# Layer 0's feed-forward gate and up products for both halves at once by Strassen's algorithm, the down blocks afterwards, and the recurrence's output transposes one chunk later

## The chip, the cores and the metric

The kernel runs on one core of a Trainium2 chip. A core has a matrix engine (TensorE, PE), two elementwise engines (VectorE, DVE, and ScalarE, ACT), a slower one (GpSimd, POOL), and SyncE (SP), which here only issues transfers (DMA). PE reads operands from on-chip memory (SBUF) and adds its products up in PSUM, which has eight banks of 128 x 512 float32. Each engine works through its own list of instructions in order and waits on semaphores. The metric is device microseconds of one execution; several executions are made and their median is given.

## The reference, cut to what matters

The computation is a two-layer trunk on 1024 positions of width 1024, in float32. Layer 0 mixes with a gated spatial mixer and pooling, layer 1 with a recurrence (RWKV-7); each layer has a SwiGLU feed-forward of hidden width 2816, which is 22 blocks of 128.

```python
def swiglu(hn, w_gate, w_up, w_down):
    return (jax.nn.silu(hn @ w_gate) * (hn @ w_up)) @ w_down

def reference(x, ...):
    h = x
    for layer in range(DEPTH):                                  # DEPTH = 2
        hn = rms_norm(h, mix_norm[layer])
        if layer % 2 == 0:
            h = h + hybrid_ab_mixer(hn, ...)
        else:
            y, v_first = rwkv7_time_mix(hn, ...)
            h = h + y
        h = h + swiglu(rms_norm(h, ffn_norm[layer]), ffn_w_gate[layer], ffn_w_up[layer], ffn_w_down[layer])
    return rms_norm(h, final_norm)

def wkv7_scan(r, w, k, v, a, b):                                # inside rwkv7_time_mix
    def step(state, inp):
        r_t, w_t, k_t, v_t, a_t, b_t = inp
        sa = jnp.einsum('bhvk,bhk->bhv', state, a_t)
        state = (state * w_t[:, :, None, :] + sa[..., None] * b_t[:, :, None, :]
                 + v_t[..., None] * k_t[:, :, None, :])
        return state, jnp.einsum('bhvk,bhk->bhv', state, r_t)
    ...
```

The feed-forward and the projections look at each position alone. The recurrence goes through the positions in order.

## The kernel before

**Precision.** Every dense operand is split into a high and a low part (`split`, line 142: ACT makes the high part, DVE subtracts it from the source and rounds the rest). A product is three matmuls, high·high, high·low and low·high (`mm3`, lines 343 to 346), each 128 x 128 by 128 x 512.

**Halves.** The positions are two halves, A (0) and B (1), of 512 columns. The residual stream `H[h]` lies transposed, as eight tiles of 128 features by 512 positions. The recurrence of layer 1 takes half A first and then half B, in eight chunks of 64 positions each.

**Weights.** `plan` lists all blocks of weights (512 KB each) in the order of use, together with the reloads of activations from DRAM. `take` (line 131) hands the next one out, splits it and loads the two after it, through three raw buffers (`raw`, tag of the pool `wst`) and three pairs of split ones. The loads are issued from ACT's queue, other transfers from SP's.

**Feed-forward.** `ffn` (line 648) goes through groups of two or three hidden blocks: for each block the gate product (24 matmuls), the up product (24), SiLU and multiplication and the split of the hidden block; then the down products of the group (24 matmuls per block), whose sums are added to `H` (`residual`, line 423). So each half of layer 0 loads and splits all gate, up and down weights for itself.

**Stages.** After layer 0's mixer: (1) all 22 blocks of half A's feed-forward, with the norm of half B, which is written to DRAM for later (`n_d`), beside it. (2) The first four blocks of half B's, with the splits and mixes for half A's layer-1 projections beside them (`beside`, line 695; `LOWRANK_AT`, `GATE_AT` and `MIX_AT` say from which step the parts come). (3) The projections of half A (`project`, line 896): gate output, keys, receptances, the inversion of the chunks' small triangular matrices on DVE, then values. (4) Half A's recurrence (`recur`, line 1152) with blocks 4 to 19 of half B's feed-forward interleaved (`drive`, line 732, ratio 3), then blocks 20 and 21 while half A's recurrence output is reloaded. (5) Half B's norm and projections, beside half A's output projection and two blocks of layer 1's feed-forward; half B's recurrence beside more of that; the rest.

**The recurrence.** Each chunk is a `burst` (line 1277) of small matmuls, all recorded at line 1176 and kept in their order on PE by `ordered` (line 1172), with ACT and DVE copies between them; within a burst the next chunk's gram products, transposes and small solves are made too. After every second chunk `post` (line 1336) normalises the output of the pair (`bn_stats` on DVE, a power on POOL, 16 ACT instructions, multiplication and addition on DVE and POOL), turns it on PE (line 1384), gates it on DVE (line 1390) and stores it (`y_d`, line 1394).

**Order.** The program is traced in the order of the code; a planner then puts every engine's instructions in order by a priority (the place in the program, 450 places earlier for the interleaved side work), by what is ready in its own model of time, and by what room in the pools is free. A tile's room is taken again when its last reader is done, by later pools too.

## Time and profile before

| | |
|---|---|
| median of 3 runs | 2477.68 us (2475.45 to 2480.0) |
| profiled execution, its own time | 2477.63 us |
| its span, first to last instruction | 2475.9 us |
| PE, DVE, ACT, POOL busy | 97%, 56%, 37%, 10% |
| mean granted clock of TensorE | 0.989 |
| moved by DMA | 310.69 MB, mean 125 GB/s |

The time is a little longer than the span, since it holds what lies around the first and the last instruction. Busy time is the union of an engine's instructions; the duration of one matmul is longer than the distance between two, since they overlap, so for dense work the count in a stretch of time says more than the duration. "Idle before, releaser" in a group says what the engine last waited for. The granted clock is 1.00 at full speed; the profile shows it at half speed for a few microseconds after some gaps in PE's work.

### The profile page before, as it was taken

How to read it: one execution, taken by the hardware profiler on the slowest of the kernel's cores; microseconds unless marked ns; L12 is line 12 of the kernel's file. 1: busy time of each engine (PE TensorE's matmuls, PEld its weight loads, DVE VectorE, ACT ScalarE, POOL GpSimd, SP SyncE). 2: the span in 40 equal slices, each digit the busy share in tenths (PEclk: the TensorE clock that was granted, in tenths of full speed). 3: DMA queues.
4: the chain of work that ended last, by engine and by line, in shares of the span. 5: the costliest groups of instructions: out<-in, count | busy, mean ns of one | idle time of the engine just before them, and what ended most of it. 6: DMA issues, size and time to landing. Idle time of an engine off the chain costs nothing.

```text
span 2475.9 us, 37980 instructions
## 1 busy us (share of the span) xinstructions
PE 2406.4 (97%) x15735; PEld 1977.5 (80%) x15735; DVE 1382.7 (56%) x2126; ACT 912.1 (37%) x1369; POOL 244.6 (10%) x262
## 2 busy tenths in 40 slices
PE   8999999999999998999999999989999999999998
PEld 7888888888878787888878777778878778888887
DVE  6445634444875874655548847856555446444443
ACT  6233422222664432432325754433232324322223
POOL 0200000000014400211000133201111000000001
PEclk9999999999999999999999999999999999999999
DMA  5123433323355577542434465695444322433231
GB/s 179 49 60 89 150 102 102 119 86 94 109 176 139 140 208 202 156 127 70 135 112 143 153 168 134 191 234 140 119 128 128 111 85 75 147 102 118 87 98 56
DMA packets 436396, 310.69 MB, mean 125 GB/s; under 512 B 93376, under 2 KB 395584, under 8 KB 435456
## 3 DMA queue, kind: packets, MB, share of 16 engines
q10 hardware_dynamic: 297280, 210.53, 28.6%
q1 hardware_dynamic: 138944, 97.75, 13.8%
q8 instruction: 123, 2.02, 0.3%
q14 instruction: 49, 0.40, 0.1%
HBM read 254.68 MB, written 53.54 MB: 124 GB/s over the span
## 4 chain that ended last, share of the span: by engine, by line
PE 82%; DMA 6%; DVE 5%; ACT 2%; issue 2%; POOL 2%; SPq 0%; ACTq 0%; POOLq 0%; DVEq 0%
PE mm L344 22%; PE mm L345 22%; PE mm L346 22%; PE sm L1176 5%; DMA raw<-y_d 1%; DVE wlo L144 1%; PE yp L1176 1%; DMA raw<-in_ffn_w_down_dram 1%; DMA lnw<-in_rwkv_ln_w_dram 1%; ACT whi L143 1%; PE aux L1097 1%; PE mm L511 1%; PE mm L512 1%; PE mm L513 1%; PE aux L1098 1%
## 5 line engine op out<-in xcount | busy, mean ns | idle before, releaser
L345 PE MATMUL mm<-alo,whi 128*128 128x512 f32 x1952 | 766.7, 393 | 0.9 <-issue 0.8
L346 PE MATMUL mm<-ahi,wlo 128*128 128x512 f32 x1952 | 765.4, 392 | 1.7 <-DVE wlo L144 1.7
L344 PE MATMUL mm<-ahi,whi 128*128 128x512 f32 x1952 | 765.8, 393 | 0.8 <-ACT whi L143 0.8
L143 ACT ACTIVATE whi<-raw 128x1024 fp32r<-128x1024 f32 x288 | 304.6, 1059 | 744.7 <-PE mm L345 605.3
L144 DVE TENSOR_TENSOR wlo<-raw,whi 128x1024 fp32r<-128x1024 f32 x288 | 359.1, 1248 | 289.5 <-ACT whi L143 270.1
L346 PEld LDWEIGHTS mm<-ahi,wlo 128*128 128x128 f32 x1952 | 367.7, 188 | 82.5 <-issue 3.5
L345 PEld LDWEIGHTS mm<-alo,whi 128*128 128x128 f32 x1952 | 367.7, 188 | 79.9 <-issue 2.9
L344 PEld LDWEIGHTS mm<-ahi,whi 128*128 128x128 f32 x1952 | 367.7, 188 | 79.0 <-issue 2.1
L344 PE MATMUL mm<-hidhi,wdhi 128*128 128x512 f32 x624 | 240.5, 395 | 8.1 <-DVE h L424 3.8
L345 PE MATMUL mm<-hidlo,wdhi 128*128 128x512 f32 x624 | 245.0, 393 | 0.4 <-DVE hidlo L674 0.4
L346 PE MATMUL mm<-hidhi,wdlo 128*128 128x512 f32 x624 | 244.9, 392 | 0.0
L424 DVE TENSOR_TENSOR h<-h,mm 128x512 f32<-128x512 f32 x192 | 129.3, 686 | 149.7 <-PE mm L346 148.5
L143 ACT ACTIVATE wdhi<-raw 128x1024 fp32r<-128x1024 f32 x82 | 86.4, 1057 | 249.7 <-DMA raw<-in_ffn_w_down_dram 164.4
L144 DVE TENSOR_TENSOR wdlo<-raw,wdhi 128x1024 fp32r<-128x1024 f32 x82 | 100.2, 1223 | 112.1 <-ACT wdhi L143 112.0
L670 DVE TENSOR_TENSOR sg<-sg,mm 128x512 f32<-128x512 f32 x88 | 60.3, 686 | 157.1 <-PE mm L346 155.3
L344 PEld LDWEIGHTS mm<-hidhi,wdhi 128*128 128x128 f32 x624 | 117.5, 189 | 36.8 <-DVE h L424 6.4
L345 PEld LDWEIGHTS mm<-hidlo,wdhi 128*128 128x128 f32 x624 | 117.8, 189 | 25.7 <-DVE hidlo L674 1.3
L346 PEld LDWEIGHTS mm<-hidhi,wdlo 128*128 128x128 f32 x624 | 117.8, 189 | 24.9
L424 DVE TENSOR_TENSOR hA<-hA,mm 128x512 f32<-128x512 f32 x72 | 48.8, 686 | 77.2 <-PE mm L346 77.0
L349 POOL TENSOR_TENSOR nrs<-nrs,small 128x4 f32<-128x4 f32 x8 | 10.0, 1244 | 667.2 <-DVE nrs L371 667.2
L674 DVE TENSOR_TENSOR hidlo<-sg,hidhi 128x512 fp32r<-128x512 f32 x88 | 65.7, 748 | 10.0 <-ACT hidhi L673 10.0
L344 PE MATMUL mm<-xhi,whi 128*128 128x512 f32 (+1 forms) x160 | 65.3, 408 | 0.0
(299 smaller groups left out, 2886.3 us busy)
## 6 DMA issues: line engine op xcount, KB each, us to landing
raw<-in_ffn_w_gate_dram ACTq DMA_DIRECT2D x88, 512.0 KB
...
```

Source lines behind the costliest of these rows:

```text
L143: act.activation(hi, src, AF.Copy)
L144: (eng or dve).tensor_tensor(out=lo, in0=src, in1=hi.bitcast(F32), op=ALU.subtract)
L344: pe.matmul(o, whi, xhi, start=first, stop=False)
L345: pe.matmul(o, whi, xlo, start=False, stop=False)
L346: pe.matmul(o, wlo, xhi, start=False, stop=last)
L424: dve.tensor_tensor(out=H[h][:, m, :], in0=H[h][:, m, :], in1=o, op=ALU.add)
L511: pe.matmul(ops[j], xhi[:, k, sl], whi[:, kk], start=(k == 0), stop=False)
L512: pe.matmul(ops[j], xhi[:, k, sl], wlo[:, kk], start=False, stop=False)
L513: pe.matmul(ops[j], xlo[:, k, sl], whi[:, kk], start=False, stop=(k == KT - 1))
L670: dve.tensor_tensor(out=s, in0=s, in1=o, op=ALU.mult)
L674: dve.tensor_tensor(out=lo, in0=s, in1=hi.bitcast(F32), op=ALU.subtract)
L1176: i = f(*args, **kw)
```

## The change

The gate and up products of layer 0 for both halves are taken as one product of 2 x 2 blocks and computed by Strassen's algorithm in Winograd's form, with seven block products in place of eight. Rows of the blocks are the two hidden blocks 2i and 2i+1 of a pair, columns the two halves, and the inner dimension is cut into k-tiles 0 to 3 and 4 to 7. With A the weights and B the normed activations:

S1 = A21+A22, S2 = S1-A11, S3 = A11-A21, S4 = A12-S2; T1 = B12-B11, T2 = B22-T1, T3 = B22-B12, T4 = B21-T2. The products A11·B11 (kept as P1), A12·B21, S2·T2, S1·T1, S3·T3, A22·T4 and S4·B22 are added up partly in PSUM, partly on DVE, to the four results.

- **First part** (`first_steps`): for the pairs 0 to 5 the products P1 and A12·B21 need half A only. They run while DVE makes the T's of `combine`; P1 is stored to DRAM (`p1_d`). Their hidden blocks are finished and stored.
- **Main part** (`full_steps`): all 11 pairs, in the order 6, 0, 7, 1, ... The weights are loaded once for both halves (those of pairs 0 to 5 a second time, half of them), summed and split on DVE and ACT (`weights`, in place in the raw buffers). Pairs 0 to 5 start from the stored P1 and need five products, the others seven. The last two products of a matrix come after the first one or two of the next. PSUM is one pool of eight banks.
- All hidden blocks go to DRAM (`hid_d`), high and low parts; the residual streams too (`hm_d`), since their room is used for the T's.
- **Down blocks** (`down_steps`): 22 for half A in groups of three; for half B four groups of three beside the projections' preparation, then groups of two: two beside half A's recurrence at ratio 28 and three after it, with the reload of its output between them. Hidden blocks come back from DRAM, `H` too.
- The norms of layer 0's feed-forward take running sums of squares as the residuals are made; half B's normed activations aren't stored and reloaded any more.
- **Recurrence**, both halves: `post` first copies the pair's output from PSUM to SBUF on ACT and normalises it there; the transposes, gating and store are put off to the next chunk's burst (`turned`).

```diff
-LOWRANK_AT, GATE_AT, MIX_AT = (5, 8), (7, 8), 2
+LOWRANK_AT, GATE_AT, MIX_AT = (2, 8), (3, 8), (1, 2)
...
-BESIDE = (4, 2)
+BESIDE = 2
+PAIRS = 11
+FIRST = (0, 1, 2, 3, 4, 5)
+PORDER = (6, 0, 7, 1, 8, 2, 9, 3, 10, 4, 5)
...
+        if key[0] in makes:
+            ready[i] = makes[key[0]](i)
+            return
         raw = raws[i]
-        hi, lo = (dest or whl)()
+        to = (dest or whl)()
+        if to is None:
+            return
+        hi, lo = to
...
+    D0A = [list(range(f, min(f + 3, 22))) for f in range(0, 22, 3)]
+    D0B = [[f, f + 1, f + 2] for f in range(0, 12, 3)], [[12, 13], [14, 15]], [[16, 17], [18, 19], [20, 21]]
+    hm_d = [dram.tile([P, KT, HT], F32, name=f"hm_d{h}") for h in range(2)]
+    hid_d = [dram.tile([P, 22, 2, HT], F32, name=f"hid_d{h}") for h in range(2)]
+    p1_d = dram.tile([P, 2 * PAIRS, HT], F32, name="p1_d")
...
+    for i, n in mats(FIRST):
+        push(("first", i, n), push_pair(0, i, n, 0))
+    for i, n in mats(PORDER):
+        for j in range(2):
+            push((f"full{j}", i, n), push_pair(0, i, n, j))
...
+    push_beside(0, [lambda g=g: push_d(0, 1, [g]) for g in D0B[0]])
+    push_proj(0)
+    push_d(0, 1, D0B[1])
+    pieces = push_act(("y", 0), y_d[0])
+    for g in D0B[2]:
+        push_d(0, 1, [g])
+        list(zip(range(2), pieces))
+    list(pieces)
...
+    FULL = {"mm": ("mm", 8)}
...
+    def quarter(o, w, x, start):
+        wh, wl = v3(w[0]), v3(w[1])
+        for k in range(4):
+            st = start and k == 0
+            pe.matmul(o, wh[:, k, :], x[0][:, k, :], start=st, stop=False, skip_group_check=True)
+            pe.matmul(o, wh[:, k, :], x[1][:, k, :], start=False, stop=False, skip_group_check=True)
+            pe.matmul(o, wl[:, k, :], x[0][:, k, :], start=False, stop=k == 3, skip_group_check=True)
...
+    def first_steps(blocks, hn, fp):
...
+        for i, n in blocks:
+            w = take(("first", i, n))
+            o = mmt()
+            quarter(o, parts_of(w, LO), b11, True)
+            t = fp.tile([P, HT], F32, tag="t1", bufs=2, name="p1")
+            act.activation(t, o, AF.Copy)
+            sp.dma_start(p1_d[:, 2 * i + n, :], t)
+            yield 0.5
+            if prev:
+                second(*prev.pop())
+                yield 0.5
+            prev.append((i, n, w, o))
+        second(*prev.pop())
+        yield 0.5
...
+    def full_steps(blocks, kept, x, fp, wp):
...
+        def weights(i):
+            (a11, a12), (a21, a22) = ((raws[j][:, LO], raws[j][:, HI]) for j in (i - 1, i))
+            s3 = wp.tile([P, HT], F32, tag="s3", bufs=1, name="s3")
+            dve.tensor_tensor(out=s3, in0=a11, in1=a21, op=sub)
+            s1, s2, s4 = a21, a11, a12
+            dve.tensor_tensor(out=s1, in0=a21, in1=a22, op=ALU.add)
+            dve.tensor_tensor(out=s2, in0=s1, in1=a11, op=sub)
+            b = whl()
+            split(s2, *parts_of(b, HI))
+            split(s1, *parts_of(b, LO))
+            d = [wp.tile([P, HT], F32R, tag=t, bufs=1, name=t) for t in ("s3hi", "s3lo")]
+            split(s3, *d)
+            dve.tensor_tensor(out=s4, in0=a12, in1=s2, op=sub)
+            c = [wp.tile([P, D], F32R, tag=t, bufs=2, name=t) for t in ("chi", "clo")]
+            split(a22, *parts_of(c, LO))
+            split(s4, *parts_of(c, HI))
+            return b, c, d
...
+        for i, n in blocks:
+            k = i in kept
+            a = mmt()
+            w = take(("full0", i, n))
+            if not k:
+                quarter(a, parts_of(w, LO), x["b11"], True)
+                t1 = tile_("t1")
+                act.activation(t1, a, AF.Copy)
+                yield 0.5
+                o = mmt()
+                quarter(o, parts_of(w, HI), x["b21"], True)
+                dve.tensor_tensor(out=t1, in0=t1, in1=o, op=ALU.add)
+                finish(i, n, 0, t1)
+                yield 0.5
+            b, c, d = take(("full1", i, n))
+            quarter(a, parts_of(b, HI), x["t2"], k)
+            yield 0.5
+            if prev:
+                prev[0]()
+                yield 0.5
+            if k:
+                t1 = tile_("t1")
+                sp.dma_start(t1, p1_d[:, 2 * i + n, :])
+            def now(t, k=k, a=a, t1=t1):
+                if k:
+                    dve.tensor_tensor(out=t, in0=t1, in1=a, op=ALU.add)
+                else:
+                    act.activation(t, a, AF.Copy)
+            u2, u3 = tile_("t2"), tile_("t3")
+            now(u2)
+            o = mmt()
+            quarter(o, parts_of(b, LO), x["t1"], True)
+            yield 0.5
+            if prev:
+                prev[1]()
+                yield 0.5
+            quarter(a, d, x["t3"], False)
+            now(u3)
+            dve.tensor_tensor(out=u3, in0=u3, in1=o, op=ALU.add)
+            finish(i, n, 3, u3)
+            yield 0.5
+            def last(i=i, n=n, k=k, a=a, t1=t1, c=c, now=now):
+                quarter(a, parts_of(c, LO), x["t4"], False)
+                if k:
+                    now(t1)
+                    finish(i, n, 2, t1)
+                else:
+                    finish(i, n, 2, tile_("t4"), a)
+            def last2(i=i, n=n, o=o, u2=u2, c=c):
+                quarter(o, parts_of(c, HI), x["b22"], False)
+                dve.tensor_tensor(out=u2, in0=u2, in1=o, op=ALU.add)
+                finish(i, n, 1, u2)
+            prev = last, last2
+        for go in prev:
+            go()
+            yield 0.5
+    def down_steps(l, h, groups, fp, nw, nh, after=None, between=iter(())):
+        dests["d0"] = lambda: (fp.tile([P, D], F32R, tag="wdhi", bufs=nw, name="wdhi"),
+                               fp.tile([P, D], F32R, tag="wdlo", bufs=nw, name="wdlo"))
+        def load(g):
+            res = {}
+            for f in g:
+                res[f] = fp.tile([P, 2, HT], F32R, tag="hd", bufs=nh, name="hd")
+                sp.dma_start(res[f].bitcast(F32), hid_d[h][:, f])
+            return res
+        nxt = load(groups[0])
+        for gi, g in enumerate(groups):
+            wd, hid = {}, nxt
+            for f in g:
+                if f == groups[-1][-1]:
+                    split_at(pos[0])
+                    dests["d0"] = None
+                wd[f] = take(("d", l, h, f))
+            if gi + 1 < len(groups) and nh >= len(g) + len(groups[gi + 1]):
+                nxt = load(groups[gi + 1])
+            for m in range(KT):
+                o = mmt()
+                ms = slice(m * P, (m + 1) * P)
+                for i, f in enumerate(g):
+                    mm3(o, wd[f][0][:, ms], wd[f][1][:, ms], hid[f][:, 0, :], hid[f][:, 1, :], i == 0, i == len(g) - 1)
+                residual(m, h, o)
+                if after is not None and gi == len(groups) - 1:
+                    after(m)
+                yield len(g) / 8
+            if gi + 1 < len(groups) and nh < len(g) + len(groups[gi + 1]):
+                nxt = load(groups[gi + 1])
+            for _ in range(2):
+                next(between, None)
...
+                if turned:
+                    turned.pop()()
...
-            yp = ypair[0]
+            ysb = wt("ysb", 1, [P, 2, 8, 64])
+            for r in range(2):
+                act.activation(ysb[:, r], ypair[0][:, r], AF.Copy)
...
+            def turn_out():
+                for q in range(2):
...
+                sp.dma_start(y_d[h][:, :, jj * P : (jj + 1) * P], gch)
+            turned.append(turn_out)
...
+        turned.pop()()
+        yield 1.0
...
+    drive(first_steps(mats(FIRST), hnA, f), combine(norm_bcast(acc[0])), 1.6)
+    for e in (rp_es, hb_es, ps_es):
+        e.close()
+    ps_es = open_psum("psf0", FULL)
+    wp, wp_es = open_pool(name="wp", bufs=1, side="left")
+    exhaust(full_steps(mats(PORDER), FIRST, x, f, wp))
+    for e in (wp_es, f_es, xt_es, actp_es, ps_es):
+        e.close()
...
+    for h, pl in ((0, ha_pool), (1, hb_pool)):
+        H[h] = pl.tile([P, KT, HT], F32, tag="h", name="h")
+        sp.dma_start(H[h], hm_d[h])
+    f, f_es = open_pool(name="ffn0d", bufs=1, side="right")
+    acc, add = running_sums(0)
...
-    drive(ffn(0, 0, hnA, f), early_work())
+    drive(down_steps(0, 0, D0A, f, 6, 6, add), wa1())
...
-    beside(0, ffn(0, 1, hnB, f, G0B[0], nd=2, after=spill_b), weights_of(G0B[0]), parts)
+    beside(0, down_steps(0, 1, D0B[0], f, 4, 3, spill_b), [len(g) for g in D0B[0]], parts)
...
-    drive(ffn(0, 1, nxt["hn"], f, G0B[1]), with_reload(hb_pool, 1, h_d[1, 0], recur(0, wp)), RATIO)
+    H[1] = hb_pool.tile([P, KT, HT], F32, tag="h", name="h")
+    for k in range(0, KT, 2):
+        sp.dma_start(H[1][:, k : k + 2, :], h_d[1, 0][:, k : k + 2, :])
+    drive(down_steps(0, 1, D0B[1], f, 3, 4), recur(0, wp), 28.0)
...
-    drive(ffn(0, 1, nxt["hn"], f, G0B[2], after=spill_h, between=take_act(("y", 0))))
+    drive(down_steps(0, 1, D0B[2], f, 3, 4, spill_h, take_act(("y", 0))))
```

## The prediction, made before the change was run

> **What bounds the kernel now.** I read the page first (engine shares, chain of waits), then busy time by stretches of time, then the groups of instructions, then the timeline around the first half's recurrence.

> ```profile
> span 2475.9 us, 37980 instructions
> PE 2406.4 (97%) x15735; PEld 1977.5 (80%) x15735; DVE 1382.7 (56%) x2126; ACT 912.1 (37%) x1369; POOL 244.6 (10%) x262
> PE 82%; DMA 6%; DVE 5%; ACT 2%; issue 2%; POOL 2%; SPq 0%; ACTq 0%; POOLq 0%; DVEq 0%
> ```

> TensorE (PE) is busy 97% of the span, and 82% of the chain that ends last is PE work. So whatever takes matmuls away is worth their time, and whatever uncovers a wait costs its length. What one matmul is worth is not its duration: matmuls overlap.

> ```profile
> L345 PE MATMUL mm<-alo,whi 128*128 128x512 f32 x1952 | 766.7, 393 | 0.9 <-issue 0.8
> 350.00:600.00 250.00, 250.00 (x1104) 207.02 (x1103) 105.20 (x123) 61.31 (x74) 0.00 (x0) 1.00 0.31 95
> ```

> The columns of a stretch are PE, weight load, DVE, ACT and POOL busy time with instruction counts, granted clock, DMA share, GB/s. One matmul lasts 393 ns, but 1104 of them go through 250 us of pure feed-forward work: 0.2264 us each. DVE is at 42% there and ACT at 25%, so this stage has room beside PE. The profiled execution took 2477.63 us, the span plus 1.7; the median of the runs is 2477.68, so the sum below is made from 2477.6.

> **What the change removes.** Layer 0's gate and up products are 22 hidden blocks x 2 matrices x 2 halves x 8 k-tiles x 3 passes (hi·hi, hi·lo, lo·hi) = 2112 matmuls. After it there are 11 pairs x 2 matrices x 7 products x 4 k-tiles x 3 passes = 1848. The down blocks keep 1056. That is 264 x 0.2264 = **-59.8 us**. Bounds: none of the seven products can be skipped, and each is the same 128x512 form, so the count is exact; only its exposure is open.

> **What it adds on DVE and ACT**, beside PE:

> ```profile
> L144 DVE TENSOR_TENSOR wlo<-raw,whi 128x1024 fp32r<-128x1024 f32 x288 | 359.1, 1248 | 289.5 <-ACT whi L143 270.1 <-PE mm L346 6.1 <-PE mm L344 5.0
> L358 DVE TENSOR_TENSOR nacc<-nacc,nsq 128x512 f32<-128x512 f32 x35 | 24.1, 687 | 0.8
> L424 DVE TENSOR_TENSOR h<-h,mm 128x512 f32<-128x512 f32 x192 | 129.3, 686 | 149.7 <-PE mm L346 148.5
> L674 DVE TENSOR_TENSOR hidlo<-sg,hidhi 128x512 fp32r<-128x512 f32 x88 | 65.7, 748 | 10.0 <-ACT hidhi L673 10.0
> 660.00:710.00 50.00, 50.00 (x221) 40.61 (x220) 46.47 (x67) 38.01 (x57) 2.55 (x4) 1.00 0.37 113
> ```

> While the first six pairs run their two products of half A (288 matmuls, 65 us of PE), DVE makes the five activation sums: per k-tile 13 operations of about 0.69, so 52 x 0.69 = 36 us, plus 12 weight splits x 1.25 = 15, plus 6 hidden blocks x 1.43 = 9: 60 us under 65.
> In the main part a matrix of a kept pair has 60 matmuls, 13.6 us. DVE does 4 weight sums (L358's 0.69) and 5 half splits (0.69), 6.2 us, and on the results 5 additions (L424's 0.686) and on average 1.5 x (0.69+0.75), 5.6 us: 11.8, or 87%. A matrix of the other pairs has 84 matmuls, 19.0 us, and 12.5 us of DVE. The last row is a stage of the kernel before in which DVE was busy 93% and PE never idle, so I take **0**, and PE's own work is the cover. The other end: the weights of a matrix need both raw blocks, there are three raw buffers, and the second load waits until the sums of the matrix before are done in place.

> ```profile
> 1172.56 0.35 ACTq L113 DMA_DIRECT2D raw<-in_ffn_w_down_dram  x1
> 1176.15 1.06 ACT L143 ACTIVATE wdhi<-raw 128x1024 fp32r<-128x1024 f32 x1 [2.78 <-DMA raw<-in_ffn_w_down_dram]
> ```

> A load is there 3.6 us after its issue. If DVE did all 11.8 us before it, the cycle would be 15.4 against 13.6, 1.8 x 12 kept matrices = 22 us. Bounds 0 to 22.

> **Hidden blocks by way of DRAM.** 44 stores and 44 loads of 0.52 MB go onto SP's queue; half of the down weights' traffic is doubled. A down group of three is 72 matmuls, 16.3 us, and wants 3.1 MB, 193 GB/s.

> ```profile
> 940.00:950.00 10.00, 6.25 (x54) 4.92 (x54) 2.82 (x5) 2.60 (x3) 0.00 (x0) 0.98 1.14 299
> 720.00:730.00 10.00, 8.37 (x24) 6.26 (x25) 1.23 (x1) 4.74 (x8) 0.00 (x0) 0.66 0.83 248
> ```

> 299 GB/s were moved in one stretch, so steady state fits. The starts do not all fit. At the start of half A's down blocks the residuals H come back from DRAM (2 x 2.1 MB) into the room of the activation tiles, which the last product still reads; the hidden blocks' tiles lie where t4 is read one product (12 matmuls, 2.7 us) earlier. Low end 2 us (hidden blocks issued first, one weight split of 1.06 + 1.25 left). High end 21 us (both H first: 5.8 MB at 299 GB/s, then the split). Nearer the low end, since what is free first can be issued first on SP: **+5**. The residual of the first tile waits for H, and PE has five PSUM tiles, 45 matmuls or 10 us, before that reaches it.
> At half B's first stage there are three hidden-block buffers for groups of three, so the next group's loads start when the group before has been read: 3.6 us for the first and 1.7 for each of two more, 7 us, once; the two later boundaries have the low-rank and gate products (48 matmuls, 10.9 us each) over them. Bounds 0 (low-rank pulled forward) to 2.3 + 2 x 7 = 16. I take **+7**.

> **The clock.** After the idle before 720 us the granted clock was 0.66, and 24 matmuls took 8.37 us in place of 5.4: 2.9 us more. Two new gaps of over 4 us in dense work: **+6**, bounds 0 to 4 gaps, 12.
> [...]

> **The recurrence of half A loses its cover.** This is the largest cost. Before, 16 hidden blocks of half B's feed-forward (1152 matmuls) run beside it, and 2 more after it. Now four down blocks (96 matmuls, 21.7 us) are interleaved at a ratio of 28, and six (144 matmuls, 32.6 us) come after it in program order.

> ```profile
> 900.00:1300.00 400.00, 387.68 (x3946) 320.69 (x3945) 220.47 (x395) 128.21 (x213) 38.24 (x32) 0.99 0.48 137
> 900.00:1200.00 300.00, 89.87 (x2654) 80.74 (x2654) 0.99 0.53 148
> 905.54 0.39 PE L1099 MATMUL mm<-whi,xlo 128*128 128x512 f32 x1
> 960.35 0.24 PE L1176 MATMUL sm<-XT,w 32*32 32x32 f32 x2
> 978.46 0.69 PE L1176 MATMUL sm<-XT,w 32*32 32x32 f32 x32
> 989.75 0.69 PE L1176 MATMUL sm<-XT,gt 32*32 32x32 f32 x32
> 1155.45 1.15 PE L1176 MATMUL yp<-uv,gt 128*64 128x64 f32 x31
> 1162.02 2.91 POOL L349 TENSOR_TENSOR var<-var,small 128x16 f32<-128x16 f32 x1 [38.81 <-DVE var L1362]
> 1165.24 4.83 ACT L1370 ACTIVATE ysb<-yp,mean,var 128x64 f32<-128x64 f32 x16 [15.51 <-DVE mean L1364]
> 1177.44 0.93 PE L1176 MATMUL sm<-ident,ysb 128*128 128x128 f32 x7
> 1181.17 0.53 SPq L1394 DMA_DIRECT2D y_d<-gch  x1
> ```

> The second row counts the recurrence's own instructions (line 1176) alone: 90 us. With 54 us of down blocks the new region holds 144 us of PE work. Its chain of latency: from the last value product (905.5) to the first burst (960.4) 55 us, of which two splits of reloaded activations leave, 52; eight bursts of 12.0 (978.46 to 990.44), 96; from the last product (1156.6) to the issue of the last y (1181.7) 25, less 3.6 for which the transposes stood behind dense matmuls, 21.5; then y's landing, reload and split, 3.6 + 2.3 + about 2: 29 in all. Each earlier pair's normalisation is a 4.83 us block on ACT in front of the next burst's copies; three of them, half hidden: 7. Sum 184, idle 184 - 144 = 40. The region before idled 400 - 387.7 = 12, so **+26 to 28; I take +26**.
> That the output transposes come a chunk later is what keeps the POOL power, the ACT block and the additions (1162.0 to 1173.7) out of the ordered PE chain; without it each pair would add some 12 us. Behind each later transpose nothing waits but the store of y.
> Low end 0: the planner hides as much as before. High end: all four normalisations exposed (+12), and groups 18 to 21, whose weights follow y's pieces in the list of loads, run only after y is there (96 matmuls, +22): 60.
> In the second half's recurrence, which keeps its cover, the later transposes can only free PE from waits, and the norm of half B isn't written out and reloaded any more: **-1**, bounds -5 to +2.

> Sum: -59.8 + 0 + 5 + 7 + 6 + 26 - 1 = -16.8: **2461 us**.

> **Rivals.**
> (1) *All covered.* The list of dense work is filled in wherever PE waits, as in the bursts shown, the region idles 12 us as before, no gap reaches the clock. For it: 97% busy in all stages of before. Against: 144 us of work cannot fill 184. -59.8 + 2 + 2.3 = 2422 us.
> (2) *Slower: the recurrence bare.* Place: from half B's last value product to its first output product. Price 60 in place of 26, the other terms as they are: -59.8 + 60 + 17 = +17, 2495 us. It decides from 43 us in this region. For it: the order of weights and y in one ring of three buffers; the first burst waited for a DMA share above 1.0. Against: PE's order already mixes single matmuls of several stages.
> (3) *Strassen's own feeding binds.* DVE and the raw ring in the kept pairs: +22, 2483 us, about the time of before or a little over. For it: 87% of DVE and a chain of split, sum, split. Against: the stage at 93%.
> That the change does not do what it says is no rival: the matmul count follows from the code.

> **From cases to numbers.** A measurement of this kernel tells about 0.2% (5 us) from no change. Forecast 0.48, its own range 2445 to 2475; (1) 0.18; (2) 0.20; (3) 0.14. Faster: 0.48 x 0.97 + 0.18 + a seventh of (3) = 0.67. Same: nearly half of (3) and the edges of the others, 0.09. Slower: 0.24. The range goes from (1) to (2), 2422 to 2495.

> **What would show it.** PE instructions of the dense kind fall by 264 and the matmul rate in the new stage stays 4.4 per us: the first step right. DVE near 85% with PE never idle in kept pairs: no cost there; PE waiting for DVE weight halves: rival (3). A PE gap before half A's first down product, waiting for H or the hidden blocks, and one between half B's first and second group. From the last value product to the first output product some 185 us with about 40 idle; 155 with 12 is rival (1), 215 or more rival (2). Wrong altogether if the gap is elsewhere, for instance at the value projection or in half B's recurrence, whose instructions hardly change.

## The result, and the profile after

The changed kernel takes 2533.1 us (median of 4 runs, 2527.9 to 2539.0), the kernel before on the same chip 2478.4 (2475.5 to 2480.0): a ratio of 1.0224, 95% interval 1.0203 to 1.0246. It is 55 us slower; 17 us faster was forecast. The profiled execution took 2539.0 us, a span of 2537.3 plus 1.7, against 2477.6 before: 61.4 us more, and it is this difference that the rows below account for.

The page of the changed kernel: the span, and the engines' busy time.

```profile
span 2537.3 us, 38209 instructions
PE 2369.7 (93%) x15471; PEld 1948.5 (77%) x15471; DVE 1493.2 (59%) x2380; ACT 953.1 (38%) x1479; POOL 237.3 (9%) x262
```

There are 264 matmuls fewer, as counted. But busy time fell by 36.7 us where 264 x 0.2264 = 59.8 are gone, so the matmuls that are left take 23.1 us longer; and idle time grew from 69.5 to 167.6 us, by 98.1. -59.8 + 23.1 + 98.1 = +61.4. Two questions follow: where the idle time stands, and why matmuls take longer.

Busy time by stages of the kernel before (columns as in the prediction: PE, weight load, DVE, ACT, POOL, granted clock, DMA share, GB/s): up to half A's gate and up; half A's feed-forward; from half A's norm to its last value product; its recurrence with what runs beside it, up to the first output product; the rest.

```profile
0.00:262.90 262.90, 254.13 (x1144) 207.95 (x1145) 136.76 (x199) 108.50 (x169) 22.11 (x49) 0.99 0.30 94
262.90:628.00 365.10, 365.10 (x1614) 302.04 (x1614) 166.72 (x200) 103.01 (x128) 5.44 (x5) 1.00 0.36 112
628.00:905.90 277.90, 267.00 (x1511) 217.67 (x1510) 209.89 (x336) 147.31 (x216) 61.95 (x63) 0.98 0.53 147
905.90:1307.90 402.00, 389.68 (x3954) 322.13 (x3953) 221.96 (x394) 130.20 (x218) 38.24 (x32) 0.99 0.49 140
1307.90:2475.90 1168.00, 1130.44 (x7519) 927.74 (x7517) 647.40 (x998) 423.07 (x640) 116.82 (x113) 0.99 0.43 126
```

The changed kernel: up to gate and up; the seven products; the gap behind them; half A's down blocks; the hand-over to half B's; half B's blocks beside half A's gates and projections; the recurrence's region; the rest.

```profile
0.00:258.70 258.70, 248.57 (x1126) 203.04 (x1127) 134.22 (x196) 106.89 (x168) 21.08 (x48) 0.99 0.34 110
258.70:685.50 426.80, 422.94 (x1859) 346.98 (x1857) 292.83 (x450) 172.35 (x281) 1.12 (x2) 1.00 0.42 134
685.50:703.30 17.80, 0.21 (x1) 0.24 (x2) 5.43 (x6) 3.58 (x4) 0.00 (x0) 0.63 0.97 369
703.30:825.20 121.90, 121.61 (x528) 100.14 (x528) 64.29 (x83) 22.02 (x23) 5.03 (x4) 0.98 0.55 192
825.20:868.00 42.80, 23.12 (x83) 17.71 (x84) 36.31 (x54) 22.76 (x33) 1.59 (x2) 0.76 0.46 169
868.00:1129.80 261.80, 255.01 (x1464) 208.75 (x1463) 185.22 (x304) 123.28 (x179) 57.75 (x61) 0.99 0.55 158
1129.80:1362.50 232.70, 161.96 (x2898) 137.38 (x2898) 131.43 (x292) 70.27 (x143) 34.28 (x32) 0.84 0.54 163
1362.50:2537.30 1174.80, 1136.23 (x7518) 934.23 (x7516) 643.49 (x1000) 432.00 (x650) 116.48 (x113) 0.98 0.43 126
```

Length minus PE's busy time is the idle time of a stage:

| place | idle before | idle after | difference |
|---|---|---|---|
| up to gate and up | 8.8 | 10.1 | +1.3 |
| the seven products (before: half A's feed-forward) | 0.0 | 3.9 | +3.9 |
| gap before half A's down blocks | none | 17.6 | +17.6 |
| half A's down blocks | none | 0.3 | +0.3 |
| half A's norm, gates, projections; in the changed kernel from the hand-over on | 10.9 | 19.7 + 6.8 | +15.6 |
| half A's recurrence, up to its first output product | 12.3 | 70.7 | +58.4 |
| the rest | 37.6 | 38.6 | +1.0 |

**The seven products** cost next to nothing beside their matmuls: 1859 in 422.9 us are 0.2275 each. Of the 3.9 us of idle time, 3.0 are six waits for the split of S3 on ACT.

**The gap before the down blocks**, first on the queue of SP, then on PE:

```profile
685.09 0.32 SPq L1815 DMA_DIRECT2D h<-hm_d  x1
685.50 0.38 SPq L728 DMA_DIRECT2D hid_d<-hid  x1
685.97 0.38 SPq L1815 DMA_DIRECT2D h<-hm_d  x1
688.24 0.32 SPq L728 DMA_DIRECT2D hid_d<-hid  x1
688.61 7.31 SPq L876 DMA_DIRECT2D hd<-hid_d  x6
```

```profile
703.09 0.76 PE L384 MATMUL mm<-hd,wdhi 128*128 128x512 f32 x1 [17.81 <-DMA hd<-hid_d]
```

Both residuals (`h`, 4.2 MB) are issued ahead of the last hidden block's store and of all hidden blocks' loads (`hd`).

**The hand-over** is what the prediction did not have at all. The kernel before went from half A's feed-forward into half B's, whose activations lay in SBUF. Now the next dense work is half B's down blocks, and they stand behind half A's norm. The waits of PE, 822 to 870 us (total, times, longest):

```profile
PE mm L384 <- ACT ahi L155: 9.3, 1, 9.3
PE aux L419 <- DVE nacc L411: 5.4, 1, 5.4
PE mm L384 <- DMA hd<-hid_d: 3.2, 1, 3.2
PE aux L432 <- DVE ndg L428: 2.1, 1, 2.1
```

In order of time they are the sums of squares (5.4), the norm's spread over the partitions (2.1), the start of half B's first down blocks (9.3) and their second group of hidden blocks (3.2). The 9.3 us are put down to a split of the normalised half A (`ahi`), but the first hidden block ended them. SyncE (SP) waited until DVE had normalised half A (`hn`) before it issued that load:

```profile
SPq L876 <- DVE hn L1057: 8.9, 1, 8.9
```

```profile
841.83 1.27 SPq L876 DMA_DIRECT2D hd<-hid_d  x3
```

The load's last part landed at 845.48 by the semaphore's record in the trace, and PE began at 845.62; the first weight's split was done at 843.1.

**The recurrence's region**: PE's waits from 1129 to 1363 us, and its two largest gaps in the tail, behind the last product of the recurrence (1302.4):

```profile
PE sm L1435 <- DMA bk<-bk_d: 14.0, 1, 14.0
PE mm L384 <- ACT wdhi L155: 12.8, 1, 12.8
PE sm L1433 <- DVE ysb L1638: 11.5, 1, 11.5
PE mm L384 <- DVE h L478: 10.6, 3, 6.3
```

```profile
1313.92 0.44 PE L1433 MATMUL sm<-ident,ysb 128*128 128x128 f32 x1 [11.53 <-DVE ysb L1638]
1332.28 0.79 PE L384 MATMUL mm<-hd,wdhi 128*128 128x512 f32 x1 [12.82 <-ACT wdhi L155]
```

The region takes 232.7 us, against the 184 that the prediction had for its chain and 215 for its worst rival. Behind the last product PE waits for the normalisation, then for down weights that were loaded behind pieces of y, and the last four blocks' 96 matmuls run only then.

**The clock.** Stretches of 3.41 us around the end of the recurrence; behind POOL's count stands the granted clock:

```profile
1294.43:1297.85 3.42, 2.58 (x50) 2.39 (x48) 0.69 (x1) 0.31 (x1) 0.13 (x1) 0.50 0.36 102
1297.85:1301.26 3.41, 3.41 (x70) 3.29 (x68) 0.69 (x1) 0.59 (x1) 0.00 (x0) 0.54 0.31 94
1301.26:1304.67 3.41, 1.13 (x40) 0.99 (x35) 2.84 (x14) 1.09 (x2) 0.00 (x0) 0.96 0.03 7
1304.67:1308.09 3.42, 0.00 (x0) 0.00 (x0) 1.50 (x12) 0.00 (x0) 1.74 (x1) 0.50 0.00 0
...
1331.98:1335.39 3.41, 3.11 (x8) 2.49 (x9) 1.23 (x1) 1.26 (x2) 0.00 (x0) 0.54 0.78 273
1335.39:1338.81 3.42, 2.62 (x12) 1.80 (x10) 2.33 (x2) 1.10 (x2) 0.00 (x0) 1.00 0.76 249
```

Behind a stretch with 1.13 us of PE work the clock is half here (1304.67), and it is full again behind stretches with 3.41 and 3.11 us of work at the slow clock (1301.26, 1335.39); behind one with 2.58 us it stays half (1297.85). The first down products after the tail (1332 to 1335) go at half speed, eight in 3.1 us. In sum the trace has the clock at half for 57 us before and 173 us after, and PE is busy in 46 us of the one and 98 of the other. At half clock one dense matmul follows another after 0.426 us (846.61 to 850.02, eight of them) in place of 0.226, so the 52 us more of slow work hold about 25 us of loss. That is an estimate, but it has the size of the 23 us.

### The profile page after: what moved, and what is told of

It is laid out like the page before. It is cut to its first block, busy times and chain, and to the rows that moved or that the text cites. A ratio compares the mean times of both kernels' runs of the same rounds, so it can differ in the third digit from the quotient of the medians.

```text
span 2537.3 us, 38209 instructions
## 1 busy us (share of the span) xinstructions
PE 2369.7 (93%) x15471; PEld 1948.5 (77%) x15471; DVE 1493.2 (59%) x2380; ACT 953.1 (38%) x1479; POOL 237.3 (9%) x262
## 5 line engine op out<-in xcount | busy, mean ns | idle before, releaser
L384 PE MATMUL mm<-ahi,whi 128*128 128x512 f32 x1248 | 489.1, 393 | 1.8 <-DVE h L478 1.0
L386 PE MATMUL mm<-ahi,wlo 128*128 128x512 f32 x1248 | 489.1, 392 | 1.4 <-DVE wlo L156 1.4
L385 PE MATMUL mm<-alo,whi 128*128 128x512 f32 x1248 | 490.2, 393 | 0.1
L155 ACT ACTIVATE whi<-raw 128x1024 fp32r<-128x1024 f32 (+1 forms) x262 | 256.7, 984 | 556.8 <-PE mm L385 404.2
L156 DVE TENSOR_TENSOR wlo<-raw,whi 128x1024 fp32r<-128x1024 f32 (+1 forms) x262 | 298.7, 1143 | 185.4 <-ACT whi L155 159.2
L384 PEld LDWEIGHTS mm<-ahi,whi 128*128 128x128 f32 x1248 | 234.6, 188 | 52.6 <-issue 1.8
L386 PEld LDWEIGHTS mm<-ahi,wlo 128*128 128x128 f32 x1248 | 234.7, 188 | 52.3 <-DVE wlo L156 2.2
L385 PEld LDWEIGHTS mm<-alo,whi 128*128 128x128 f32 x1248 | 234.7, 188 | 51.4 <-issue 1.9
L384 PE MATMUL mm<-hd,wdhi 128*128 128x512 f32 x352 | 144.4, 411 | 58.1 <-DMA hd<-hid_d 25.5
L385 PE MATMUL mm<-hd,wdhi 128*128 128x512 f32 x352 | 143.0, 406 | 0.0
L386 PE MATMUL mm<-hd,wdlo 128*128 128x512 f32 x352 | 138.0, 398 | 0.0
L715 PE MATMUL mm<-ahi,whi 128*128 128x512 f32 x264 | 103.4, 392 | 0.7 <-ACT p L750 0.7
L716 PE MATMUL mm<-alo,whi 128*128 128x512 f32 x264 | 102.7, 389 | 0.0
L717 PE MATMUL mm<-ahi,wlo 128*128 128x512 f32 x264 | 101.8, 389 | 0.0
```

Of the source, the lines that this page charges most:

```text
L155: act.activation(hi, src, AF.Copy)
L156: (eng or dve).tensor_tensor(out=lo, in0=src, in1=hi.bitcast(F32), op=ALU.subtract)
L384: pe.matmul(o, whi, xhi, start=first, stop=False)
L385: pe.matmul(o, whi, xlo, start=False, stop=False)
L386: pe.matmul(o, wlo, xhi, start=False, stop=last)
L715: pe.matmul(o, wh[:, k, :], x[0][:, k, :], start=st, stop=False, skip_group_check=True)
```

## The experiments

All are variants of the changed kernel (2533.1 us) unless said; ratios are against the kernel before, with 95% intervals. From one kernel to the next line numbers move by a few.

### The gap before the down blocks

`hid_first` moves the text: the hidden blocks' loads, then half A's residuals in four pieces; half B's later.

```
-        sp.dma_start(H[h], hm_d[h])
...
+    pre = load_hid(0, D0A[0], f, 6)
...
+    for k in range(0, KT, 2):
+        sp.dma_start(H[0][:, k : k + 2, :], hm_d[0][:, k : k + 2, :])
...
     def wa1():
         yield 8.0
+        sp.dma_start(H[1], hm_d[1])
```

> Against the changed kernel (2533). Where half A's down blocks start, the hidden blocks of the first group are loaded ahead of the residuals, half A's residuals follow in four pieces, and half B's are loaded later beside the down blocks. Theory A (both residuals first on the queue set the 17.8 us gap, at half clock afterwards): the gap falls to 6 to 9 us and the time by 9 to 13, to about 2522. Theory B (the split of the first weight, which needs room that the last product still reads, or the DMA engines set it): the gap stays above 14 us and the time within 4 us of the changed kernel.

Measured: 2535.2, 1.0228 (1.0206 to 1.0250). The gap is as before (17.5 us), but this decides neither theory: what stands later in the text is still first on the queue of SP, since the planner sets the order:

```profile
685.26 0.32 SPq L1826 DMA_DIRECT2D h<-hm_d  x1
...
688.85 10.33 SPq L871 DMA_DIRECT2D hd<-hid_d  x6
```

`hid_after` ties the order (`tc.issue_after`: issued behind, without a wait):

```
     for k in range(0, KT, 2):
+        with tc.issue_after(last_hd[0]):
             sp.dma_start(H[0][:, k : k + 2, :], hm_d[0][:, k : k + 2, :])
...
+        with tc.issue_after(last_hd[0]):
+            sp.dma_start(H[1], hm_d[1])
```

> Against the changed kernel (2533). In the run before, the new order of the text did not change the order on the queue: the residuals were still issued at 685.3 us, ahead of the last hidden block's store (688.4) and of the hidden blocks' loads (688.9), and the first weight split waited for that store until 695. Here the residuals are tied behind the loads of the first group's hidden blocks (half A's at once behind them, half B's behind those of the third group). Theory A (4.2 MB of residuals in front of one store and three loads set the gap): gap 17.8 to about 7 us, time -9 to -13, about 2522. Theory B (the load and split of the first weight, or the loads' own latency): the gap stays above 14.

Measured: 2533.3, 1.0218 (1.0193 to 1.0243). The gap on PE in `hid_after`, and in each kernel the time from the first down product to the end, the changed kernel first:

```profile
694.73 0.77 PE L384 MATMUL mm<-hd,wdhi 128*128 128x512 f32 x1 [8.11 <-DMA hd<-hid_d]
```

```profile
703.30:2537.30 1834.00, 1697.93 (x12488) 1398.20 (x12488) 1060.73 (x1729) 670.32 (x1027) 215.14 (x212) 0.96 0.47 141
```

```profile
694.70:2536.90 1842.20, 1700.05 (x12488) 1397.11 (x12488) 1061.95 (x1729) 670.08 (x1027) 215.02 (x212) 0.96 0.48 143
```

Theory A holds at its place, 17.8 to 8.1 us: the order on the queue made more than half of the gap. In the total the gain is not seen. The rest, with the same 12488 matmuls, took 8 us longer, 6 of it idle: a kernel is planned as a whole, and the order further on came out differently. A stage's gain in one of these kernels is no gain in time until the medians show it.

### The hand-over

`hand`: half A's last and half B's first down blocks share one pool for weights and hidden blocks, every other group of half A's hidden blocks lies in a second pool (`fx`), the residuals are tied as above, and half B's first group is multiplied ahead of half A's norm.

```
-    f, f_es = open_pool(name="ffn0d", bufs=1, side="right")
+    f, f_es = open_pool(name="ffn0d", bufs=1, side="left")
...
+    fx, fx_es = open_pool(name="ffn0x", bufs=1, side="right")
...
-    drive(down_steps(0, 0, D0A, f, 6, 6, add), wa1())
-    f_es.close()
+    drive(down_steps(0, 0, D0A, f, 4, 6, add, h1_later(), pre, fx), wa1())
+    fx_es.close()
...
+    blocks_b = down_steps(0, 1, D0B[0], f, 4, 3, spill_b)
+    for _ in range(KT):
+        next(blocks_b)
     hn1 = project_norm(0, np_, norm_bcast(acc[0]))
```

> Against the changed kernel (2533). As the run with the residuals behind the hidden blocks, and half A's last down blocks and half B's first ones share their rooms for weights and hidden blocks, so that half B's first group is loaded and multiplied ahead of half A's normalisation. Theory A (between 825 and 868 us TensorE had nothing but work behind that normalisation): the 20 us of idle and 12 of half clock there fall below 5 and 4, the time by about 30 in all, 2503. Theory B (the stage after it is bound by VectorE's or ScalarE's mixes, so what is won here is lost before the projections): no more than the 10 us of the first gap.

Measured: 2521.1, 1.0167 (1.0143 to 1.0192): 12 us won, nearer to theory B's 10 than to theory A's 30. In place of the four waits above (20.0 us) two are left, 2.6 and 1.9 us, so theory A has the place right. But from the first down product to half A's last value product PE's idle time fell by 12.2 us (26.4 to 14.2) and the length by 7.6 only (426.3 to 418.7): PE is now busy for 28 us at half clock there, against 19, and so longer with the same matmuls.

### Half A's recurrence

`h_prio` reloads half B's residuals with a high priority, so that they stand ahead of the recurrence's loads.

```
+    with tc.high_priority(offset=2 * AHEAD):
         for k in range(0, KT, 2):
             sp.dma_start(H[1][:, k : k + 2, :], h_d[1, 0][:, k : k + 2, :])
```

> Against the changed kernel (2533). At the start of half A's recurrence half B's residuals are reloaded ahead of the recurrence's own loads instead of behind them; before, the third down tile waited for them until 1161 us. Theory A (the residuals' place in the queue holds the dense work back): TensorE has its down products in the 14 us in which it waited for the first chunk's loads, the time falls by 5 to 10 us. Theory B (the DMA engines are full from 1130 to 1170 us, so what is loaded first only delays what is loaded second): the first burst comes 6 us later and the time is within 5 us of the changed kernel, or up to 6 us more.

Measured: 2528.8, 1.0200 (1.0183 to 1.0218); the interval overlaps the changed kernel's, so a gain is not certain. PE still waits for them, 12.1 us. It isn't the queue that held them back: SP waited 5.4 us for the store of the triangular inverse (`xi_d<-xi`) before it issued them, so their room wasn't free; `s7e` will change that.

`y_last` loads all down weights ahead of y, and takes y's pieces behind all products.

```
-    pieces = push_act(("y", 0), y_d[0])
-    for g in D0B[2]:
-        push_d(0, 1, [g])
-        list(zip(range(2), pieces))
-    list(pieces)
+    push_d(0, 1, D0B[2])
+    list(push_act(("y", 0), y_d[0]))
...
-    drive(down_steps(0, 1, D0B[2], f, 3, 4, spill_h, take_act(("y", 0))))
+    drive(down_steps(0, 1, D0B[2], f, 3, 4, spill_h))
+    exhaust(take_act(("y", 0)))
```

> Against the changed kernel (2533). In the changed kernel the last four down weights of half B stand behind pieces of y in the list of loads, and TensorE waits 12.8 us for the first of them after the last transposes. Here all six weights stand ahead of y. Theory A (order of loads): the 96 matmuls of the last two groups move into the bursts or under the last normalisation; from the last product of the recurrence (1302.4) to the first output product the 60 us shrink to about 30 (transposes until 1319.5, then y's landing and split), and the time falls by 25 to 30 us to about 2505. Theory B (the chain of the recurrence or the loads bind whatever the order): the idle time moves into the bursts, less than 8 us are won, 2525 or more.

Measured: 2539.5, 1.0236 (1.0216 to 1.0255). Theory A falls. Bursts and tail of the changed kernel, then of `y_last`:

```profile
1160.90:1302.40 141.50, 121.76 (x2670) 106.20 (x2668) 87.20 (x202) 44.63 (x102) 27.63 (x25) 0.92 0.48 144
1302.40:1362.30 59.90, 27.99 (x105) 21.58 (x106) 31.28 (x63) 21.05 (x34) 5.43 (x3) 0.72 0.44 142
```

```profile
1163.80:1329.20 165.40, 145.11 (x2764) 122.22 (x2764) 106.03 (x229) 53.10 (x114) 28.19 (x26) 0.93 0.48 147
1329.20:1370.30 41.10, 6.10 (x19) 4.18 (x20) 25.34 (x60) 17.98 (x35) 6.45 (x4) 0.56 0.41 131
```

The 96 matmuls went into the bursts, which grew by 24 us: more than their own 21.7. The bursts' idle time did not shrink (19.7 and 20.3 us).

`y_hold` is `y_last` and keeps them out of the bursts by tying their hidden blocks' loads behind the last load of the normalisation.

```
+    late_f = {(1, f) for f in range(18, 22)}
...
+            with tc.issue_after(held[0]) if (h, f) in late_f else ExitStack():
                 last_hd[:] = [sp.dma_start(res[f].bitcast(F32), hid_d[h][:, f]).ins]
```

> Against the changed kernel (2533). As the run in which the last four down weights stand ahead of y (there all 240 products were done before the recurrence's last product, whose bursts grew by 24 us, and TensorE idled 34 of the last 40 us). Here the hidden blocks of the last four are loaded only behind the last load for the normalisation, so that their 96 products (21.7 us) are left for the time after the recurrence's last product. Theory A (a burst has its own 12 to 15 us of TensorE work and hides only some 3 us beside it, while the 37 us after the last burst are empty): bursts as in the changed kernel, 142 us, tail 40, time -15 to -22, about 2515. Theory B (the loads come too late or the output chain is slowed by the products between): less than 6 us.

Measured: 2551.0, 1.0289 (1.0264 to 1.0313), worse. Most of the products (79 of 96) are in the tail now and PE is busy in 23 of its 45 us, but the tail's length is y's and the output weights': PE's longest wait there is 13.2 us for the first output weight's split, whose load stands in the ring of three buffers behind y's pieces. And the bursts took 162 us, 20 more than in the changed kernel, with 19 dense products more in them; why so much wasn't tried.

`bare` has no products beside the recurrence: all 22 of half B's blocks stand beside half A's gates.

```
-    D0B = [[f, f + 1, f + 2] for f in range(0, 12, 3)], [[12, 13], [14, 15]], [[16, 17], [18, 19], [20, 21]]
+    D0B = [D0A]
...
-    drive(down_steps(0, 1, D0B[1], f, 3, 4), recur(0, wp), 28.0)
+    drive(iter(()), recur(0, wp), 28.0)
```

> Against the changed kernel (2533). All 22 down blocks of half B stand beside half A's gates, none beside its recurrence: the region from the last value product to the first output product then shows the recurrence's own chain with nothing beside it. The prediction had 184 us for it (startup 52, eight bursts of 12.0, tail and normalisations 36). Theory A (a burst alone is 15 to 18 us, not 12.0, as the bursts without products beside them in the runs so far suggest): region 200 to 215 us; the stage before it grows by 54 us, so the time is 25 to 35 us above the changed kernel. Theory B (the chain is as predicted, and what makes the region long is the products beside it and the loads behind them): region 175 to 188 us, the time about that of the changed kernel.

Measured: 2587.2, 1.0427 (1.0398 to 1.0456). Start, bursts and tail of the recurrence alone:

```profile
1205.10:1239.60 34.50, 7.06 (x106) 5.78 (x106) 9.32 (x23) 3.92 (x9) 3.12 (x5) 0.61 0.88 233
1239.60:1361.10 121.50, 98.33 (x2544) 90.28 (x2544) 68.72 (x180) 43.71 (x103) 25.76 (x24) 0.86 0.48 136
1361.10:1404.70 43.60, 6.30 (x23) 3.96 (x19) 25.29 (x60) 17.99 (x35) 6.45 (x4) 0.56 0.40 123
```

Its own chain is 199.6 us, at the edge of theory A's range: start 34.5, a burst 121.5 / 8 = 15.2, tail 43.6. The changed kernel puts 240 matmuls, 54.3 us, beside it and needs 232.7: only 199.6 + 54.3 - 232.7 = 21 us of them are hidden. (The chain's 199.6 us hold the half clock too: it is granted 0.75 of the clock there.) The kernel as a whole lost more than theory A said (54 us in place of 25 to 35); the stage before the recurrence, given 54 us of matmuls, grew by some 75.

### More products beside the recurrence

`s1` is `hand` and `h_prio` together (both edits as above).

> Against the changed kernel (2533). Two edits together: the shared rooms that took the hand-over between half A's and half B's down blocks away (measured 2521 alone), and half B's residuals reloaded ahead of the recurrence's loads (measured 2529 alone). Theory A (each shortens its own place): the gains add, 2515 to 2518. Theory B (the fixed order of the instructions passes small gains on as longer bursts): 2521 or more.

Measured: 2513.4, 1.0133 (1.0116 to 1.0150): the gains add, theory A.

`s2` moves four blocks from beside the gates to beside the recurrence.

```
+    D0B = [[f, f + 1] for f in range(0, 8, 2)], [[f, f + 1] for f in range(8, 18, 2)], [[18, 19], [20, 21]]
...
-    drive(down_steps(0, 1, D0B[1], f, 3, 4), recur(0, wp), 28.0)
+    drive(down_steps(0, 1, D0B[1], f, 3, 4), recur(0, wp), 11.2)
```

> As the kernel with both edits, and four of the twelve down blocks that stood beside half A's gates are moved beside its recurrence, which then has fourteen blocks (336 products, 76 us) in place of ten (240, 54 us). Theory A (what the region lacks is cover: its chain of 185 us and more is there whatever runs beside it): the stage of gates and projections shortens by 22 us, the region grows by less than 8, and the time falls by 14 to 20 against the kernel without the move. Theory B (the planner puts the products where the bursts are, which have their own 12 to 15 us of TensorE work, and the head and tail of the recurrence stay empty): the region grows by 15 to 22 us and nothing is won.

Measured: 2502.6, 1.0095 (1.0080 to 1.0110): 11 us less than `s1`, a little under theory A. The place is theory A's: in the profiled runs the stage from half A's first down product to its last value product is 22 us shorter (418.8 to 396.3), and the region is 233 us as in `s1` (232).

`s3` is `s2` with the load order of `y_last` (the same edit).

> As the run before with fourteen blocks beside the recurrence, and all down weights ahead of y in the list of loads. Theory A (with fourteen blocks there are products left for the 37 us after the last burst, and with the weights first they can run there): 8 to 15 us less than the run before. Theory B (as with ten blocks: the products are done in the bursts, the tail is empty): the same as the run before within 5 us, or more.

Measured: 2516.1, 1.0148 (1.0133 to 1.0163), 13 us more than `s2`: theory B, as with ten blocks.

`s4` is `s2` with two edits in the tail: y's pieces get a room of their own, out of the weights' ring (loaded from SP's queue), and the last four blocks' products are tied on PE behind the recurrence's last product.

```
+    y_raw = [yr.tile([P, D], F32, tag="yr", bufs=4, name="yr") for _ in range(4)]
+    for i in range(4):
+        sp.dma_start(y_raw[i].rearrange("p (k t) -> p k t", k=2), y_d[0][:, 2 * i : 2 * i + 2, :])
...
+                with tc.issue_after(held_pe[0]) if hold else ExitStack():
                     for i, f in enumerate(g):
```

> Against the kernel with fourteen blocks beside the recurrence (2502.6). The pieces of y no longer share the ring of three weight buffers: they are loaded into a room of their own, and the last four blocks' products are tied behind the recurrence's last product, so that they stand where TensorE waited 11 us for the normalisation and 13 us for the weights behind y. Theory A (those two waits are what is left of the tail): from the last recurrence product to the first output product 43 us becomes about 30 with 96 products in it, the time falls by 10 to 15, to about 2490. Theory B (the output chain, normalisation, transposes, y's way through DRAM and its split, takes its 40 us however it is filled, or the recurrence's bursts take the loss): less than 5 us.

Measured: 2478.4, 0.9994 (0.9979 to 1.0009): 24 us less than `s2`, and no different from the kernel before. Start, bursts and tail:

```profile
1087.90:1134.00 46.10, 30.93 (x219) 24.25 (x221) 24.33 (x43) 8.32 (x11) 3.13 (x5) 0.85 0.99 308
1134.00:1278.70 144.70, 127.10 (x2682) 111.12 (x2676) 94.01 (x209) 50.79 (x109) 25.80 (x24) 0.89 0.58 166
1278.70:1308.60 29.90, 25.68 (x113) 19.95 (x114) 23.40 (x59) 13.75 (x29) 6.54 (x4) 0.98 0.41 136
```

The tail is 30 us, 44.0 in `s2`, and PE is busy in 26 of them, at full clock. The region takes 220.7 us with 336 matmuls (76.1 us) in it: against `bare`'s chain 55 us of them are hidden. That chain had y in the ring; how long it is with y in its own room wasn't run, so part of the 55 may be a shorter chain. Which of the two edits does how much wasn't run either; `y_hold`, tied but with y in the ring, points to the ring. And not all of the 24 us are the tail's 14: from the first output product to the end, where no edit reaches, the profiled run of `s4` takes 1166.5 us and that of `s2` 1177.2. PE's order differs there. These 11 us are luck; `s7` below has the opposite.

`s5` and `s6` move two and four blocks more (and set the ratio from 11.2 to 9.3); in `s6` the last six stand behind the recurrence.

```
+    D0B = [[0, 1], [2, 3], [4], [5]], [[f, f + 1] for f in range(6, 18, 2)], [[18, 19], [20, 21]]
```

```
+    D0B = [[0], [1], [2], [3]], [[f, f + 1] for f in range(4, 16, 2)], [[16, 17], [18, 19], [20, 21]]
```

> Against the last kernel, with fourteen blocks beside half A's recurrence and y in its own room (2478.4). Two more down blocks move from beside the gates to beside the recurrence: sixteen blocks, 48 products or 10.9 us moved. In the kernel before this one the last four bursts have almost no products beside them (17 us each, 15.6 us idle in sum, 24 us at half clock). Theory A (cover is still short): the stage before shortens by 11 us, the region grows by 3 to 6, 2470 to 2474, faster than the kernel before. Theory B (a burst hides only 3 us, so what is moved is paid twice as often as it is hidden): within 3 us of 2478.

> As the run with sixteen blocks beside the recurrence, but eighteen, and six in place of four of them behind the recurrence's last product. Theory A: another 3 to 6 us less than that run, about 2468. Theory B (the products in the tail outlast the output chain, which is then what waits, and VectorE, 80% busy beside the gates, begins to bind there): 2476 or more.

Measured: `s5` 2497.6, 1.0069 (1.0049 to 1.0090); `s6` 2502.7, 1.0090 (1.0067 to 1.0114). Theory B, and more than it. The stage of gates and projections in `s4`, then in `s5`:

```profile
877.70:1087.90 210.20, 201.05 (x1214) 163.05 (x1212) 160.29 (x275) 105.11 (x158) 57.21 (x61) 0.98 0.54 150
```

```profile
877.90:1088.60 210.70, 194.38 (x1169) 155.25 (x1167) 158.55 (x268) 108.07 (x162) 59.03 (x59) 0.97 0.53 143
```

It lost 48 matmuls and none of its length: PE's idle time there grew from 9 to 16 us, so what is moved out of it isn't won. Which engine's chain it is wasn't tried. Of the 21 us between the two profiled runs 12 lie in the region (232.8 for 220.7), which has the 48 matmuls now, and 8 behind it.

`s7e` reorders a pool, so that half B's residuals are reloaded where tiles lay that are done before the triangular inverse's; `s7` also lets half A's first hidden blocks use the rooms that come free first, with half A's blocks in nine groups.

```
+        w2 = tmp("w2", 1, [P, D], F32R), tmp("a2", 1, [P, D], F32R)
+        early.update(cum=[tmp("cum", 1)], em=[tmp("em", 1)], av=[tmp("av", 2)])
         early.update(xi=[tmp("xi", 1, [P, 32, 2, 32])], iat=[tmp("iat", 1, [P, 32, 32])], it=[tmp("it", 1, [P, 256])])
```

```
+    D0A = [[f, f + 1, f + 2] for f in range(0, 15, 3)] + [[15, 16], [17, 18], [19, 20], [21]]
...
-    pre = load_hid(0, D0A[0], f, 3)
+    pre = load_hid(0, D0A[0], fx, 3)
```

> Against the kernel with fourteen blocks and y in its own room (2478.4). Half B's residuals, reloaded at the start of half A's recurrence, lie where the tiles of the triangular inverse lay, whose store is the last thing of the stage before; TensorE waited 11 us for them at 1109. Here tiles that are done earlier lie there. Theory A (the room is what the reload waits for): the wait shrinks to 3 us or less, 4 to 8 us are won, about 2471, faster than the kernel before (2480). Theory B (the DMA engines, full from 1090 us on, bring them no earlier, or the fixed order passes the gain on): within 4 us of 2478.

> As the run before, and half A's first group of hidden blocks goes into the rooms that are free 5 us earlier (half A's down blocks in nine groups for it), so that its loads no longer stand behind the last stores on the queue. Theory A: the gap before half A's down blocks, 8.6 us, becomes 4 to 5, another 3 to 5 us less, about 2467. Theory B (nine groups cost VectorE eight more additions, or the gain is passed on): within 3 us of the run before.

Measured: `s7e` 2484.8, 1.0024 (1.0015 to 1.0034); `s7` 2488.1, 1.0037 (1.0024 to 1.0050). Both waits shrank where they were aimed at, 11.0 to 7.6 us and 8.2 to 3.2, and the time rose by 6 and 10 us. In `s7e` SP no longer waits for the inverse's store (6.1 us in `s4`), so the room was what held the reload's issue; but PE's wait for hidden blocks beside it grew from 4.6 to 8.4 us, and the two together stayed (15.6 and 16.0). In `s7` the first gap's gain is lost later. From half B's last value product on, which no edit touches, `s4` and `s7` take:

```profile
1614.50:2474.80 860.30, 836.36 (x5912) 690.20 (x5910) 417.88 (x634) 269.66 (x415) 52.11 (x49) 0.99 0.40 117
```

```profile
1610.50:2485.20 874.70, 840.09 (x5914) 693.16 (x5912) 416.79 (x635) 269.79 (x416) 51.56 (x49) 0.99 0.39 115
```

14 us apart with the same work, 11 of it idle time. In half B's recurrence the planner put a different number of dense products into the same bursts: PE's order there differs. In `s7e`, where dense and small products follow each other as in `s4`, the same stretch took 865.0 us, so some 5 us of such a difference are the scatter of single executions. So the losses were undone down to the old time, but not turned into a gain: none of these kernels beats the kernel before.

### The later output transposes

`tr_now` undoes the later transposes alone, and leaves the copy of the pair's output to SBUF; `b_later` makes both, the copy and the later transposes, in the kernel before; `s4t` undoes the later transposes in `s4`.

```
-                if turned:
-                    turned.pop()()
...
-            turned.append(turn_out)
+            yield 0.3
+            turn_out()
```

> Against the changed kernel (2533). Only the later output transposes are undone: they follow the normalisation of their pair at once. Theory A (they keep the normalisation's 12 us out of the ordered chain, which has little cover left in half A): 20 to 40 us slower, most of it in half A's bursts, which grow from 16 us to over 20 on average. Theory B (the planner fills what stands between): within 6 us of the changed kernel.

> The kernel before with one part of the change alone: its output transposes come a chunk later (and the normalisation reads a copy of the recurrence's result). Theory A (with dense work beside it the recurrence hides either order): within 4 us of 2478. Theory B (the later transposes and the added copies cost time of their own): 5 us or more slower, in both halves' recurrences alike. Theory C (they free TensorE's ordered chain from the normalisation also here): 4 to 10 us faster.

> The kernel with fourteen blocks and y in its own room (2478.4), with the output transposes at once again. In the changed kernel this cost 19 us, in the kernel before the later transposes themselves cost 7 us. Theory A (what the later transposes are worth depends on how much cover the recurrence has; here it is between the two): between 4 us faster and 10 us slower. Theory B (half A's ordered chain with four bare bursts pays for every normalisation that stands in it): 10 to 19 us slower.

Measured: `tr_now` 2552.5, 1.0290 (1.0273 to 1.0308), 19 us more than the changed kernel; `s4t` 2498.9, 1.0070 (1.0050 to 1.0091), 20 more than `s4`; `b_later` 2486.4, 1.0029 (1.0020 to 1.0038), 7 more than the kernel before. PE's waits in the bursts of `s4t`:

```profile
PE sm L1437 <- DVE ysb L1639: 25.3, 2, 15.0
PE sm L1437 <- POOL ysb L1639: 6.7, 2, 3.3
```

With little beside the recurrence each transpose in PE's fixed order waits for its pair's normalisation; a chunk later it doesn't: `s4`'s bursts have no such wait, and they are 22 us shorter. With the kernel before's 1152 products beside the recurrence the step and its copies cost 7 us. Theory A of `tr_now` holds, at its lower edge, and theory B of `s4t`, a little beyond its upper one. For `b_later` the size is theory B's; its place is not, since half B's recurrence and all behind it took 5 us less, and the loss lies from half A's recurrence to half B's projections: in the same 393.9 us of half A's recurrence PE did 58 matmuls fewer and was idle for 18.2 us in place of 12.3, and what was left over made the next stage 12 us longer. Whether the order or the copies lose there wasn't tried.

## Why the prediction was wrong

The largest step that failed is the term for half A's recurrence: a chain read off a stretch in which it was filled, and all work beside it counted as hidden. Next are the hand-over and the clock. In the order of the sum:

- **Count, -59.8: right.** 15735 to 15471 matmuls, at 0.2275 us each in the new stage.
- **DVE and the weights' ring, 0 (0 to 22): right.** 3.9 us idle in 427, DVE at 293 of 427 us (69%, not near 85). Rival (3) is out.
- **Start of half A's down blocks, +5 (2 to 21): 17.6.** The step that failed is "what is free first can be issued first on SP". With the order tied it was (`hid_after`, 8.1 us); left to the planner it wasn't. The high end, both residuals first, is what the queue shows, and `hid_after` confirms the cause. (The down weights are loaded 88 times in both kernels; that half of their traffic is doubled is not so, but nothing was summed from it.)
- **Half B's first boundary, +7: 3.2**, in the row of the hand-over's waits.
- **The hand-over: no term.** The prediction costed what each new stage needs at its start, but not that the old neighbour, half B's gate and up, had been the cover of half A's norm. 15.6 us idle more, the 3.2 of the boundary in them; `hand` won 12 us from this and the gap before.
- **The clock, +6 (0 to 12): 23.** The term was two gaps of 2.9 us. The clock is half for 116 us more, and 68 of them lie in the recurrence's region, where PE is busy in part and which the prediction had left out of this term.
- **Half A's recurrence, +26 (0 to 60): +58.4**, and with the half clock more. Two readings failed. "Eight bursts of 12.0" was taken between two marks inside a burst (from one burst to the next the same marks are 18.1 us apart, 960.35 to 978.46); alone a burst takes 15.2. "Idle 184 - 144" let every matmul beside the chain hide in it; 21 of 54 us did. The start (34.5 for 52) was too high, because the 55 us it was read from held 180 dense matmuls. The tail was too low, 43.6 for 36 with the normalisations.
- **The second half, -1 (-5 to +2): about +7.** Idle time is 1.0 us more; PE's busy time from 1362.5 on is 5.8 us more for the same matmuls, the clock again and part of the 23 above. What the later transposes do there stays open: from half B's last value product to the end the kernel before takes 864 us, `b_later` 858, the changed kernel 871 and `tr_now`, without them, 859. The plans scatter by more than the term.

Rival (2) came nearest: its place is right, its price of 60 for the region too (58), and what it named, the last groups' weights behind y, is in the trace. But `y_last` shows that this order alone isn't why the region is long. 2495 still missed, because the hand-over and most of the clock were in no case; that the price of 60 comes out is in part luck: it was made up of exposed normalisations (12) and late products (22), where the runs show longer bursts and filler that isn't hidden. The claim that the later transposes keep the normalisation out of PE's order in half A held: 19 and 20 us.
